# Weight sums of a seven-product block form, made in device memory by accumulating transfers

## The chip, the cores and the metric

The kernel runs on one core of a Trainium2 chip. The core has TensorE (PE: matrix products; PEld in the profile is its weight load), VectorE (DVE), ScalarE (ACT), GpSimd (POOL) and SyncE (SP, which here only issues transfers), each with its own queue of instructions, and 16 transfer (DMA) engines that all queues share. The metric is the device time of one execution in microseconds (us), less is better.

## The reference

Two layers of an encoder over 512 tokens of width 1024, in float32. Each layer adds three parts to x: a mixer of two kinds of attention, an attention over 256 memory tokens, and a feed-forward part. The change is in the last:

```python
def conv_ffn(h, w_up, conv_w, conv_b, w_down):
    u = h @ w_up
    up = jnp.pad(u, ((0, 0), (1, 1), (0, 0)))
    u = up[:, :-2] * conv_w[0] + up[:, 1:-1] * conv_w[1] + up[:, 2:] * conv_w[2] + conv_b
    gate, val = jnp.split(u, 2, axis=-1)
    return (jax.nn.silu(gate) * val) @ w_down

for l in range(DEPTH):                                   # DEPTH = 2
    x = x + hybrid_mixer(rms_norm(x, norm_mix[l]), w_in[l], ...)
    x = x + memory_cross_attention(rms_norm(x, norm_mem_q[l]), rms_norm(mem, norm_mem_kv[l]), ...)
    x = x + conv_ffn(rms_norm(x, norm_ffn[l]), w_up[l], conv_w[l], conv_b[l], w_down[l])
return rms_norm(x, norm_final)
```

`w_up` is 1024 x 5632: 2816 columns of "gate", then 2816 of "val". `w_down` is 2816 x 1024.

## The kernel before

Activations lie with channels on partitions: x is 8 tiles `xT` of 128 channels x 512 tokens. A float32 product is made of three products of rounded operands: each operand is split into a "hi" part (rounded, cast by ACT) and a "lo" part (the rest, a subtraction on POOL or DVE), and `mm3` multiplies hi by hi, hi by lo and lo by hi. Weights come from device memory in a fixed list, `plan`: each entry is loaded into one of three buffers `raw` by SP's queue, and split into `hi` and `lo` (four buffers each) before its use. SP issues the next load of the list when a `raw` buffer is free.

One layer takes about 620 to 650 us. First the mixer's attention runs: steps of 8 units of neighbourhood attention, then 16 of the grouped kind, with projections as filler between the steps (`weave`; `na_quanta(s)` is called once in each step s of the first kind). Then comes the attention over the memory tokens, and last the feed-forward part, in 22 chunks j of 128 gate and 128 val columns, with rows of `w_down` woven in from the second group on.

Chunks 0 to 5 are plain products. Chunks 6 to 21 ("blocks" in the text below, 16 per layer) are made by seven products of half size instead of eight. With the rows of `w_up` in two halves of 512, a11 and a12 are the upper and lower half of the gate columns and a21 and a22 those of the val columns; the tokens are in two halves of 256. The seven products need the weights a11, a12, a22 themselves and four sums of halves. Before the change the sums are made block by block from the two loaded `raw` tiles by four DVE instructions (lines 773, 774, 779 and 780), into buffers `sf`, which are then split like weights:

```python
DVE.tensor_add(both[:, :4], raw[:, :4], raw[:, 4:])                    # 773
DVE.tensor_sub(both[:, 4:], both[:, :4], sums["gate"][:, :4])          # 774
DVE.tensor_sub(both[:, :4], sums["gate"][:, 4:], sums.pop("s2"))       # 779
DVE.tensor_sub(both[:, 4:], sums["gate"][:, :4], sums["val"][:, :4])   # 780
```

The order of instructions on PE, ACT, DVE and POOL is not the written one: the class `Order` simulates the program with assumed durations and due times, and records an order for each engine (`InOrder` marks instructions that keep their written order). SP's transfers stay as written. Within an engine's queue everything runs in the recorded order: an instruction that waits holds all that are behind it.

Of the kernel before, what the change touches and what calls it, by code (L numbers as in the profile page):

```python
# [19 lines left out]
P = 128  # L20
S = 512
D = 1024
# [17 lines left out]
SCALED = 3  # L40
CUTS = 1
FIRST_ROWS = 2
# [20 lines left out]
LATE = 3600  # L63
N_SF = 2
N_RAW, N_W, N_R, N_T, N_S, AHEAD, N_WARM, N_FIRST = 3, 4, 21, 14, 24, 2, 7, (12, 24)
# [135 lines left out]

SLOTS = {"r": N_R, "t": N_T, "s": N_S, "mm": 4, "sc": 2, "tr": 2, "raw": N_RAW, "sf": N_SF, "hi": N_W, "lo": N_W, "xg": 2, "rep": 1}

# [8 lines left out]

DMA_ISSUE, DMA_NS, DMA_RATE, DMA_SHARE, DMA_GAP, DMA_MOST = 480.0, 2700.0, 310.0, 0.5, 150.0, 8

ROUNDS, REPLAYS, MARGIN, SHARES, STRETCH, SEED = 12, 4, 100.0, (0.0, 0.0, 0.5, 1.0, 2.0), 500, 4
# [9 lines left out]
class Step:  # L225
# [5 lines left out]
    def __init__(self, ins, index):  # L231
        self.ins, self.index, self.engine = ins, index, self.ENGINES[ins.engine]
        self.dma = type(ins).__name__ == "InstDMACopy"
        self.reads, self.writes = ([p for p in map(self.part, v) if p] for v in (ins.ins, ins.outs))
        self.names = list(dict.fromkeys(p[0] for p in self.writes + self.reads))
        self.bytes = 4.0 * self.count(ins.outs[0].bass_ap.ap) if self.dma else 0.0
        if self.dma and self.reads:

            self.bytes *= 1.5 if self.writes else 0.4
        self.busy, self.takes = self.times()  # L240
        self.sharing = self.shares()

    @staticmethod
# [6 lines left out]
    @classmethod  # L250
    def part(cls, arg):

        ap = getattr(arg, "bass_ap", None)
        if ap is None or not isinstance(ap.tensor, tile.Tile):
            return None
        row, dims = 1, [tuple(d) for d in ap.ap]
        for n in ap.tensor.shape[1:]:
            row *= n
        p0, at = divmod(ap.offset, row)
# [19 lines left out]
    def shares(self):  # L279

        what = type(self.ins).__name__
        if self.engine == "POOL":
            return bool(self.wide(self.reads)) and getattr(self.ins, "op", None) != ALU.pow
        if self.engine != "DVE" or what not in ("InstTensorTensor", "InstTensorScalarPtr") or self.banked(self.reads):
            return False
        return bool(self.reads) and max(p[4] for p in self.reads) > 1

    def times(self):

        ins, what = self.ins, type(self.ins).__name__  # L290
        if self.dma:
            return DMA_ISSUE, DMA_ISSUE
# [40 lines left out]
class Order:  # L333
# [107 lines left out]
    def due(self):  # L441

        start, now = {}, FIRST_PRODUCT
        for s in self.steps:
            if s.engine == "PE":
                start[s.index] = now - self.credit.get(s.index, 0.0)
                now += s.busy
        end = now + 1e4
        self.latest, queue = [end] * len(self.steps), end
        for s in reversed(self.steps):  # L450
            until = min([end] + [self.latest[j] - self.wait(s, self.steps[j]) for j in self.chain[s.index]])
            if s.engine == "PE":
                self.latest[s.index] = start[s.index]
            elif s.dma:
                queue = self.latest[s.index] = min(until - DMA_NS - s.bytes / DMA_RATE, queue - s.busy)
            else:
                self.latest[s.index] = min([until - s.takes] + [self.latest[j] for j in self.then.get(s.index, ())])

    def run(self, given=None, draw=None):
# [141 lines left out]
        while len(issued) < n or moving:  # L601
# [45 lines left out]
            for name in s.names:  # L647
# [4 lines left out]
                held.add(name)  # L652
            if s.dma:
                if not moving:
# [9 lines left out]
def encoder_kernel(ctx: ExitStack, tc: tile.TileContext, t: dict, out: bass.AP):  # L664
# [12 lines left out]
    spool = ctx.enter_context(tc.tile_pool(name="spool", bufs=N_S))  # L677
    psum = ctx.enter_context(tc.tile_pool(name="psum", bufs=2, space=PSUM))

    uid = [0]  # L680
# [38 lines left out]
    def raw_tile():  # L719
        key, loads, nk, ncol, eng = plan[len(raws)]  # L720
        if not loads:
            raws.append(None)
            return None, loads
        if eng[1:] == "x":
            raw = rtile((nk, ncol), F32)
        else:
            raw = wpool.tile([P, nk, ncol], F32, tag="raw", name=nm("raw"), bufs=N_RAW)
        raws.append(raw)
        return raw, loads
# [6 lines left out]
    def emit_split(act=ACT, cuts=2):  # L736
# [3 lines left out]
        raws[n] = None  # L740
        if key[0] in FORMS:
            ready.append(FORMS[key[0]](raw, act))
            return
        if key[0] in ("up", "down", "memq", "memo"):
            cuts = 1
        hi = wpool.tile([P, nk, ncol], F32R, tag="hi", name=nm("hi"))
        lo = wpool.tile([P, nk, ncol], F32R, tag="lo", name=nm("lo"))
        for i in range(cuts):
# [3 lines left out]
        ready.append((hi, lo))  # L752

    sums = {}

    def split_form(src, n, act, eng):
        hi = wpool.tile([P, 2 * n, P], F32R, tag="hi", name=nm("hi"), padded_shape=[P, KC, P])
        lo = wpool.tile([P, 2 * n, P], F32R, tag="lo", name=nm("lo"), padded_shape=[P, KC, P])
        act.copy(hi, src)  # L759
        for i in range(CUTS if eng is POOL else 1):  # L760
            c = slice(2 * n * i // CUTS, 2 * n * (i + 1) // CUTS) if eng is POOL else slice(0, 2 * n)
            eng.tensor_sub(lo[:, c], src[:, c], f(hi)[:, c])  # L762
        return hi, lo

    def form_gate(raw, act):
        sums["gate"] = raw
        return split_form(raw, 4, act, POOL)

    def form_sums(raw, act):
        sums["val"] = raw  # L770
        both = wpool.tile([P, KC, P], F32, tag="sf", name=nm("sf"), bufs=N_SF)
        sums["s2"] = both[:, 4:]
        DVE.tensor_add(both[:, :4], raw[:, :4], raw[:, 4:])
        DVE.tensor_sub(both[:, 4:], both[:, :4], sums["gate"][:, :4])  # L774
        return split_form(both, 4, act, DVE)

    def form_differences(raw, act):
        both = wpool.tile([P, KC, P], F32, tag="sf", name=nm("sf"), bufs=N_SF)
        DVE.tensor_sub(both[:, :4], sums["gate"][:, 4:], sums.pop("s2"))
        DVE.tensor_sub(both[:, 4:], sums["gate"][:, :4], sums["val"][:, :4])  # L780
        return split_form(both, 4, act, POOL)

    def form_val(raw, act):
        return split_form(sums["val"][:, 4:], 2, act, DVE)

    FORMS = {"gate": form_gate, "sums": form_sums, "diffs": form_differences, "val": form_val}

# [151 lines left out]
    qrs = [cpool.tile([P, 2 * NB], F32, name=f"qr{g}") for g in range(4)]  # L939

    def load_parameters():
        SP.dma_start(par[:, 0, 8:], t["par"][:, 0, 8:])
        SP.dma_start(par[:, 1], t["par"][:, 1])
        SP.dma_start(gfin, t["gfin"])

    ident = cpool.tile([P, P], F32, name="ident")
# [223 lines left out]
    for l in range(DEPTH):  # L1170
# [506 lines left out]

        def na_quanta(s):
            if l == 0 and s < 7:
                stat.step(1)  # L1680
# [158 lines left out]
        def convolve(j, us):  # L1839
            cs = []  # L1840
            for side in range(2):
                ch = side * NF + j
                u = us[side]
                w = [par[:, l, CW + i * 2 * NF + ch : CW + i * 2 * NF + ch + 1] for i in range(3)]
                cc = tmp()
# [42 lines left out]
        def token_forms():  # L1888


            made = {}
            for name, a, b in (("t1", (0, 1), (0, 0)), ("t2", (1, 1), "t1"), ("t3", (1, 1), (0, 1)), ("t4", (1, 0), "t2")):
                src = made[name] = rtile((4, HALF), F32)
                for i in range(2):
                    k = slice(2 * i, 2 * i + 2)
                    other = made[b][:, k] if isinstance(b, str) else quarter(*b)[i]
                    (POOL if name == "t3" else DVE).tensor_sub(made[name][:, k], quarter(*a)[i], other)
                xform[name] = hi, lo = [rtile((4, HALF)) for _ in range(2)]
                ACT.copy(hi, src)
                (POOL if name in ("t2", "t3") else DVE).tensor_sub(lo, src, f(hi))  # L1900
                yield
# [256 lines left out]
```

## Time and profile before

| | us |
|---|---|
| median of 3 runs (1311.10 to 1312.67) | 1311.57 |
| span of the profiled execution, first to last instruction | 1308.7 |
| TensorE busy in it | 1298.8 |
| DVE busy | 995.7 |
| ACT busy | 786.2 |
| POOL busy | 716.6 |

The profile is of one execution, and its span leaves out what lies around the program, so it stands 2.9 us under the median. The granted TensorE clock is 0.999 of full speed. Stages in the trace, in us from the start: attention of the first layer from about 39 to 235, memory attention to 325, its feed-forward part to 640; the second layer likewise from 640, its attention about 690 to 880, its feed-forward part from 975 to the end. "Busy" of TensorE is modelled for the ends of its matmuls, which overlap; the distance from one start to the next tells its pace. Rows of the profile name an instruction by source line, engine, operation, output<-inputs and shape, then x count, busy us and mean ns, and the idle time before it with what ended it. Rows by stretch give, behind the stretch and its length, busy us and count of PE, PEld, DVE, ACT and POOL, then the granted clock, the transfer engines' busy share and GB/s. Rows in order of time begin with the start and the length in us.

### The profile page before, as it was taken

The numbers are of one execution on the slowest core, as the hardware profiler recorded it, in microseconds if no ns is written. First come the engines' busy times: TensorE is split into PE (matmuls) and PEld (weight loads), VectorE is DVE, ScalarE is ACT, GpSimd is POOL, SyncE is SP. The second block draws the span as 40 slices with busy tenths as digits, with TensorE's granted clock in tenths as the row PEclk, the third lists the DMA queues.
The fourth block names the chain that finished last, engine by engine and source line by source line (L and its number), as shares of the span: only waits on it lengthen the run. The fifth ranks groups of instructions, "written<-read, shape, count | busy, mean of one in ns | idle before, by whom it ended". The sixth has DMA issues, their size and how long they took to land.

```text
span 1308.7 us, 20968 instructions
## 1 busy us (share of the span) xinstructions
PE 1298.8 (99%) x7595; PEld 1144.2 (87%) x7595; DVE 995.7 (76%) x1855; ACT 786.2 (60%) x1459; POOL 716.6 (55%) x518
## 2 busy tenths in 40 slices
PE   9999999999999999999999999999999999999998
PEld 8888888888789999999888888888888999999987
DVE  6559877675999888788535688776759999887874
ACT  6668876565555555555536678775645555555544
POOL 2757955727454454445746569656364544444443
PEclk9999999999999999999999999999999999999999
DMA  8734322313223433333455533223232333333341
GB/s 256 211 117 110 113 65 66 109 36 113 85 61 106 116 102 101 98 95 102 134 154 167 147 79 104 62 73 94 60 93 85 89 89 105 103 97 94 106 139 65
DMA packets 203464, 137.50 MB, mean 105 GB/s; under 512 B 5600, under 2 KB 192480, under 8 KB 203360
## 3 DMA queue, kind: packets, MB, share of 16 engines
q1 hardware_dynamic: 202944, 135.77, 35.4%
q8 instruction: 60, 0.98, 0.3%
q14 instruction: 44, 0.36, 0.1%
q10 hardware_dynamic: 416, 0.39, 0.1%
HBM read 126.18 MB, written 2.10 MB: 98 GB/s over the span
## 4 chain that ended last, share of the span: by engine, by line
PE 95%; DVE 2%; ACT 1%; issue 1%; DMA 1%; POOL 0%; POOLq 0%; SPq 0%; ACTq 0%; DVEq 0%
PE mm L104 65%; PE sc L104 22%; PE tr L104 4%; PE tr L1558 2%; PE tr L1403 1%; PE tr L1747 1%; DMA r<-in_memT 1%; DVE t L1853 0%; ACT hi L750 0%; PE tr L1473 0%; DVE r L1875 0%; DVE r L1052 0%; DVE xg L1884 0%; ACT r L1051 0%; DVE t L1461 0%
## 5 line engine op out<-in xcount | busy, mean ns | idle before, releaser
L751 POOL TENSOR_TENSOR lo<-raw,hi 128x512 fp32r<-128x512 f32 (+3 forms) x229 | 368.1, 1620 | 276.2 <-ACT hi L750 226.2
L104 PE MATMUL mm<-r,hi 128*128 128x512 f32 (+1 forms) x1344 | 387.2, 368 | 0.0
L104 PEld LDWEIGHTS mm<-r,hi 128*128 128x128 f32 x1344 | 238.0, 189 | 34.9
L104 PE MATMUL mm<-xg,hi 128*128 128x512 f32 (+1 forms) x960 | 266.3, 363 | 0.8 <-DVE xg L1884 0.4
L104 PE MATMUL mm<-r,lo 128*128 128x512 f32 (+1 forms) x704 | 251.0, 358 | 0.0
L750 ACT CAST hi<-raw 128x512 fp32r<-128x512 f32 (+3 forms) x233 | 167.5, 741 | 129.6 <-PE mm L104 39.5
L104 PEld LDWEIGHTS mm<-xg,hi 128*128 128x128 f32 x960 | 170.0, 189 | 28.0 <-ACT mm L1855 1.1
L104 PE MATMUL mm<-xg,lo 128*128 128x512 f32 (+1 forms) x480 | 173.4, 361 | 0.0
L104 PE MATMUL sc<-r,hi 128*128 128x256 f32 (+1 forms) x832 | 163.2, 292 | 0.0
L762 POOL TENSOR_TENSOR lo<-sf,hi 128x1024 fp32r<-128x1024 f32 x32 | 78.0, 2437 | 147.9 <-ACT hi L759 101.0
L104 PEld LDWEIGHTS mm<-r,lo 128*128 128x128 f32 x704 | 132.9, 189 | 20.0
L104 PEld LDWEIGHTS sc<-r,hi 128*128 128x128 f32 x832 | 133.6, 191 | 4.8
L104 PE MATMUL sc<-r,lo 128*128 128x256 f32 (+1 forms) x416 | 121.2, 292 | 0.0
L759 ACT CAST hi<-sf 128x1024 fp32r<-128x1024 f32 x64 | 67.1, 1048 | 87.6 <-DVE sf L774 38.7
L104 PE MATMUL mm<-hi,xg 128*128 128x512 f32 (+1 forms) x384 | 111.4, 360 | 0.0
L104 PEld LDWEIGHTS mm<-xg,lo 128*128 128x128 f32 x480 | 90.6, 189 | 14.1
L762 POOL TENSOR_TENSOR lo<-raw,hi 128x1024 fp32r<-128x1024 f32 x32 | 78.0, 2436 | 43.6 <-ACT hi L759 37.3
L1058 POOL TENSOR_SCALAR t<-t,s 128x512 f32<-128x512 f32 (+1 forms) x112 | 66.7, 611 | 52.4 <-DVE s L1542 28.5
L104 PEld LDWEIGHTS sc<-r,lo 128*128 128x128 f32 x416 | 79.6, 191 | 1.1
L104 PEld LDWEIGHTS mm<-hi,xg 128*128 128x128 f32 x384 | 68.1, 190 | 8.8
L104 PE MATMUL sc<-r,r 128*128 128x256 f32 (+1 forms) x352 | 73.6, 330 | 0.0
L104 PE MATMUL mm<-lo,xg 128*128 128x512 f32 (+1 forms) x192 | 68.5, 357 | 0.0
(213 smaller groups left out, 2626.8 us busy)
## 6 DMA issues: line engine op xcount, KB each, us to landing
raw<-in_w_up SPq DMA_DIRECT2D x88, 512.0 KB, 3.7
raw<-in_w_in SPq DMA_DIRECT2D x25, 512.0 KB, 4.6
raw<-in_w_down SPq DMA_DIRECT2D x32, 384.0 KB, 3.4
raw<-in_w_mem_kv SPq DMA_DIRECT2D x16, 512.0 KB, 4.2
raw<-in_w_down SPq DMA_DIRECT2D x24, 320.0 KB, 3.1
r<-in_bias SPq DMA_DIRECT2D x16, 384.0 KB, 4.7
r<-r SPq DMA_DIRECT2D x22, 256.0 KB, 3.5
raw<-in_w_in SPq DMA_DIRECT2D x18, 256.0 KB, 4.8
```

The source lines that it names most:

```text
L104: return self.engine.matmul(out, lhsT, rhs, **k)
L750: act.copy(hi[:, k], raw[:, k])
L751: (POOL if eng[0] == "P" else DVE).tensor_sub(lo[:, k], raw[:, k], f(hi)[:, k])
L759: act.copy(hi, src)
L762: eng.tensor_sub(lo[:, c], src[:, c], f(hi)[:, c])
L1058: eng.tensor_scalar(e, e, sums[:, col : col + 1], 1.0, op0=ALU.mult, op1=ALU.mult)
L1403: PE.transpose(tr[:, (2 * i + c) * P : (2 * i + c + 1) * P], es[j][:, i, c * P : (c + 1) * P], ident)
L1558: PE.transpose(tr[:, k * P : (k + 1) * P], es[j][:, k * P : (k + 1) * P], ident)
L1747: PE.transpose(tr[:, (2 * c + i) * P : (2 * c + i + 1) * P], e[:, i, c * P : (c + 1) * P], ident)
```

## The change

The sums are made once per layer and for all 16 blocks, in device memory. Two tensors per layer, `sums` and `diffs`, each 1024 x 2048, are filled half by half (512 x 2048, 4.19 MB): ScalarE's queue issues a plain copy of one half of a `w_up` part into it, and POOL's queue then issues a transfer that adds a second operand to what is there (`accum_op`). The third sum adds onto the first, so its source is the half made before. The four pairs are written in steps 0 to 3 of the neighbourhood attention of the same layer. The feed-forward part then loads `sums` and `diffs` like weights, and of the val columns only the lower half (a22). [...] The `sf` buffers go. `Order` learns of the new transfers ("far": landing 45 us after the issue, a POOL issue 1.5 us).

```diff
+    made = [[dpool.tile([D, WIDE], F32, name=f"dr_{n}{l}") for n in ("sums", "diffs")] for l in range(DEPTH)]
+    def make_form(l, n, act):
+        w, half = t["w_up"][l], D // 2
+        gate, val = slice(P * PLAIN, D_FF), slice(D_FF + P * PLAIN, 2 * D_FF)
+        sums, diffs = made[l]
+        a11, a12, a21, a22 = w[:half, gate], w[half:, gate], w[:half, val], w[half:, val]
+        dst, base, more = [(sums[:half], a21, a22), (sums[half:], a11, sums[:half]),
+                           (diffs[half:], a11, a21), (diffs[:half], a12, sums[half:])][n]
+        act.dma_start(dst, base)
+        nc.gpsimd.dma_start(dst, more, accum_op=ALU.add, max_dma_last_dim=4 * 2048)
...
         if j >= PLAIN:
             cols(("gate", j), t["w_up"][l], 0, KC, P * j, P)
-            cols(("sums", j), t["w_up"][l], 0, KC, D_FF + P * j, P)
-            plan.append((("diffs", j), [], KC, P, "P"))
-            plan.append((("val", j), [], KC, P, "P"))
+            cols(("sums", j), made[l][0], 0, KC, P * (j - PLAIN), P, "D")
+            cols(("diffs", j), made[l][1], 0, KC, P * (j - PLAIN), P)
+            cols(("val", j), t["w_up"][l], KC // 2, KC // 2, D_FF + P * j, P, "D")
...
         def na_quanta(s):
+            if s < 4:
+                make_form(l, s, ACT_IN_ORDER)
...
+                if side and j >= PLAIN:
+                    w = [minus[:, l, i, j : j + 1] for i in range(3)]
...
+                    if name == "t4":
+                        DVE.tensor_add(src[:, k], one, other)
+                    elif name == "t2":
+                        DVE.tensor_sub(src[:, k], other, one)
...
+                if name in ("t1", "t4"):
+                    ACT.mul(hi, src, -1.0)
+                    DVE.scalar_tensor_tensor(lo, src, -1.0, f(hi), op0=ALU.mult, op1=ALU.subtract)
...
+            elif s.far:
+                self.latest[s.index] = until - FAR_NS
...
-    nc = bacc.Bacc("TRN2", target_bir_lowering=False, num_devices=1, dynamic_dma_scratch_size=1024)
+    nc = bacc.Bacc("TRN2", target_bir_lowering=False, num_devices=1, dynamic_dma_scratch_size=4096)
```

How the order moves. First ScalarE's queue early in the first layer's attention, before and after; `r` here are projected values, `hi` casts of weights, `t` and `s` the softmax's tiles:

```order
L1054 ACTIVATE r_392<-mm_396,s_319 128x4x64 x2
L750 CAST hi_509<-raw_382 128x512 x2
L750 CAST hi_580<-raw_390 128x512
L1054 ACTIVATE r_393<-mm_449,s_319 128x4x64
L750 CAST hi_580<-raw_390 128x512
L1054 ACTIVATE r_393<-mm_449,s_319 128x4x64
```

```order
L1059 ACTIVATE r_401<-mm_405,s_328 128x4x64 x2
L79 DMA dr_sums_78<-in_w_up 512x2048
L784 CAST hi_520<-raw_391 128x512 x2
L784 CAST hi_591<-raw_399 128x512
L1059 ACTIVATE r_402<-mm_458,s_328 128x4x64
L784 CAST hi_591<-raw_399 128x512
L79 DMA dr_sums_78<-in_w_up 512x2048
```

The first two copies have come in, the rest stands as it was; the first of these casts starts at 39.46 us in the trace of before.

POOL's queue further on in the same attention, before and after; L1058 (after: L1063) scales softmax rows, L1468 (L1473) turns projected queries, L1078 (L1083) splits an output:

```order
L1078 TENSOR_TENSOR r_1273<-t_1050,r_1273 128x512
L1468 TENSOR_TENSOR t_1283<-t_1283,t_1282 128x8x32 x2
L1468 TENSOR_TENSOR t_1357<-t_1357,t_1356 128x8x32
L1058 TENSOR_SCALAR t_1305<-t_1305,s_1304 128x256
L1058 TENSOR_SCALAR t_1306<-t_1306,s_1304 128x256 x2
```

```order
L1083 TENSOR_TENSOR r_1290<-t_1067,r_1290 128x512
L1473 TENSOR_TENSOR t_1300<-t_1300,t_1299 128x8x32 x2
L714 DMA dr_diffs_79<-in_w_up 512x2048
L1473 TENSOR_TENSOR t_1374<-t_1374,t_1373 128x8x32
L1063 TENSOR_SCALAR t_1323<-t_1323,s_1321 128x256
L1063 TENSOR_SCALAR t_1322<-t_1322,s_1321 128x256
L1063 TENSOR_SCALAR t_1323<-t_1323,s_1321 128x256
```

The accumulating transfer of the third pair, which waits for the third copy, has come in ahead of the turning of a query and of the scalings behind it.

SP's queue in the feed-forward part of the first layer, before and after:

```order
L81 DMA raw_4773<-in_w_up 128x8x128
L81 DMA raw_4805<-in_w_down 128x6x128
L81 DMA raw_4844<-in_w_up 128x8x128
L81 DMA raw_4937<-in_w_up 128x8x128
L81 DMA raw_4969<-in_w_down 128x6x128
```

```order
L79 DMA raw_4586<-in_w_up 128x8x128
L79 DMA raw_4618<-dr_sums_78 128x8x128
L79 DMA raw_4650<-dr_diffs_79 128x8x128
L79 DMA raw_4686<-in_w_up 128x4x128
L79 DMA raw_4716<-in_w_down 128x6x128
```

A block's two loads of `w_up` (512 KB each) have become four, the last of them of half size.

More of the change, by code (lines that the diff above doesn't have):

```diff
@@ L241, in __init__, with in_dram @@
         self.sharing = self.shares()
+    @classmethod
+    def in_dram(cls, arg):
+        ap = getattr(arg, "bass_ap", None)
+        return ap is not None and isinstance(ap.tensor, tile.Tile) and cls.kind(ap.tensor.name) == "dr"
     @staticmethod
@@ L258, in part @@
             row *= n
+        if cls.kind(ap.tensor.name) == "dr":
+            first, last = ap.offset // row, (ap.offset + sum(step * (n - 1) for step, n in dims)) // row
+            return ap.tensor.name, first, last + 1 - first, 1, cls.count(dims[1:])
         p0, at = divmod(ap.offset, row)
@@ L290, in times @@
         ins, what = self.ins, type(self.ins).__name__
+        if self.dma and self.engine == "POOL":
+            return FAR_POOL, FAR_POOL
         if self.dma:
@@ L652, in run @@
                 held.add(name)
-            if s.dma:
+            if s.far:
+                landed.add(j)
+                over_(s, t, t + FAR_NS)
+            elif s.dma:
                 if not moving:
@@ L752, in emit_split @@
         ready.append((hi, lo))
[L754 to L786, printed above, removed]
     def prepare_w(ahead):
@@ L944, in load_parameters @@
         SP.dma_start(gfin, t["gfin"])
+        for i in range(DEPTH):
+            taps = par[:, i, CW : CW + 6 * NF].rearrange("p (i c) -> p i c", i=3)
+            DVE.tensor_scalar(minus[:, i], taps[:, :, NF:], -1.0, None, op0=ALU.mult)
     ident = cpool.tile([P, P], F32, name="ident")
```

42 lines of the change are left out of this document (24 added, 18 removed).

## The prediction

> **What bounds the kernel now.** I read the page's busy times first, then the busy time by stretch, then the long stretch of the feed-forward blocks (400 to 640 us) by instruction form, since the change takes work from the vector engine (DVE) there.
>
> ```profile
> PE 1298.8 (99%) x7595; PEld 1144.2 (87%) x7595; DVE 995.7 (76%) x1855; ACT 786.2 (60%) x1459; POOL 716.6 (55%) x518
> ...
> 400.00:640.00 240.00, 240.00 (x1625) 222.99 (x1624) 196.36 (x308) 127.92 (x192) 113.96 (x56) 1.00 0.34 100
> ...
> L104 PE MATMUL mm<-r,hi 128*128 128x512 f32 x280 | 86.9, 392 | 0.0
> L104 PE MATMUL mm<-r,lo 128*128 128x512 f32 x140 | 54.5, 389 | 0.0
> ...
> 408.95 1.44 PE tr L104 x12
> ...
> 619.87 20.20 PE mm L104 x89
> ```
>
> The matmul ends are modelled, so "240 of 240 us busy" alone proves little; the pitch does. The last two rows come from the chain of waits: twelve 256-wide products in 1.44 us, 0.120 us each, and 89 of 512 in 20.20 us, 0.227 us each. The stretch holds 1625 matmuls, of which 280 + 140 = 420 are 512 wide and 1205 are 256 wide (all its other forms): 420 x 0.227 + 1205 x 0.120 = 95.3 + 144.6 = 239.9 us in 240.0. TensorE waits for nothing there, and no product is added or taken. So whatever leaves DVE in these blocks is worth 0 us.
>
> **The change, part by part.** *The sums leave DVE.* Four groups go:
>
> ```profile
> L773 DVE TENSOR_TENSOR sf<-raw 128x512 f32<-128x512 f32 x32 | 60.0, 1874 | 6.8 <-DMA raw<-in_w_up 6.8
> L774 DVE TENSOR_TENSOR sf<-sf,raw 128x512 f32<-128x512 f32 x32 | 23.0, 717 | 0.1
> L779 DVE TENSOR_TENSOR sf<-raw,sf 128x512 f32<-128x512 f32 x32 | 32.6, 1019 | 0.0
> L780 DVE TENSOR_TENSOR sf<-raw,raw 128x512 f32<-128x512 f32 x32 | 21.8, 681 | 0.0
> ```
>
> That is 60.0 + 23.0 + 32.6 + 21.8 = 137.4 us of DVE, all beside a gapless TensorE: 0 us. The negated tokens and taps change operations one for one and add two small ones: 0 us, under the same cover.
>
> *More loads per block.* A block (an up-chunk j of 6 and more) now loads 0.5 + 0.5 + 0.5 + 0.25 MB where it loaded 1 MB; 32 blocks, 24 MB more. The bound there is the three "raw" buffers.
>
> ```profile
> raw<-in_w_up SPq DMA_DIRECT2D x88, 512.0 KB, 3.7
> raw<-in_w_down SPq DMA_DIRECT2D x32, 384.0 KB, 3.4
> ...
> L759 ACT CAST hi<-sf 128x1024 fp32r<-128x1024 f32 x64 | 67.1, 1048 | 87.6 <-DVE sf L774 38.7 <-PE sc L104 36.3 <-PE mm L104 7.1
> L762 POOL TENSOR_TENSOR lo<-sf,hi 128x1024 fp32r<-128x1024 f32 x32 | 78.0, 2437 | 147.9 <-ACT hi L759 101.0 <-PE mm L104 47.0
> L773 DVE TENSOR_TENSOR sf<-raw x14: 693/2098/2745, 401.0 to 602.1; 128x512 f32<-128x512 f32 x14
> ```
>
> One is held for landing, cast and subtraction: 3.7 + 1.05 + 2.44 = 7.2 us for gate and for differences, about 6.0 for sums (subtraction on DVE, half as long), under 5 for the quarter, about 6 for each of 1.3 to 1.6 w_down rows. That is 33 to 35 us per block over three buffers, 11 to 12 us; the last row's 14 blocks start 201.1/13 = 15.5 us apart. It fits with a quarter to spare: 0 us.
>
> *The sums in device memory.* Per layer four plain copies on ScalarE's queue and four accumulating transfers on POOL's, 512 x 2048 x 4 B = 4.19 MB each. Issuing costs ScalarE 8 x 0.5 us (the SP row of 50.82 us below has two issues in 1.00 us). POOL has no such row; I bound its 8 issues by that 0.5 us and by its longest row above, 2.4 us each, 4 to 19 us in all, and take the low end as the nearest in kind. The places at which they stand have 1.8 to 4.7 us of idle POOL beside them (rows below): 0 us on the path. What costs is where they run and what waits for them. No copy from device memory to device memory stands in this trace. One copy's time c, if it had all 16 transfer engines to itself, is bounded by these rows, the first three from 3.1 to 3.4 us, where the engines were full, the last two from the whole span:
>
> ```profile
> DMA packets 139, 0.11 MB, mean 362 GB/s; under 512 B 14, under 2 KB 110, under 8 KB 139
> ...
> q10 hardware_dynamic: 109, 0.05, 56.3%
> q1 hardware_dynamic: 30, 0.06, 52.5%
> ...
> q1 hardware_dynamic: 202944, 135.77, 35.4%
> q8 instruction: 60, 0.98, 0.3%
> ```
>
> At 362 GB/s c is 11.6 us. All loads together (0.354 x 1308.7 = 463 us of all engines for 135.77 MB, 293 GB/s) make it 14.3 us; the instruction queue, the one with large packets (16 KB), 3.9 us for 0.98 MB, 250 GB/s, 16.8 us. The copied rows are 8 KB long and the loads' mostly 512 B, so I go above the loads' mean, between the first two: c = 13 us. The q10 and q1 rows are the only overlap of two queues: 0.05 against 0.06 MB, half each. So I let queues share equally.
>
> *Where they run.* By the new order the first copy is issued just ahead of the first of these ScalarE rows, and in layer 1 just behind the second; the others follow within 31 us.
>
> ```profile
> 39.46 1.14 ACT L750 CAST hi<-raw 128x512 fp32r<-128x512 f32 x2 [0.54 <-PE mm L104]
> ...
> 688.66 0.61 ACT L750 CAST hi<-raw 128x512 fp32r<-128x512 f32 x1
> ...
> 39.00:62.00 23.00, 23.00 (x122) 19.71 (x121) 10.51 (x30) 16.80 (x41) 17.93 (x19) 1.00 0.90 250
> 62.00:82.00 20.00, 20.00 (x113) 17.33 (x112) 13.19 (x38) 12.16 (x35) 10.68 (x13) 1.00 0.63 197
> 82.00:110.00 28.00, 28.00 (x158) 24.30 (x157) 19.59 (x57) 18.82 (x51) 21.13 (x23) 1.00 0.49 142
> 690.00:720.00 30.00, 30.00 (x156) 25.51 (x156) 17.26 (x47) 19.20 (x49) 18.82 (x21) 1.00 0.59 182
> 734.00:757.00 23.00, 22.70 (x126) 19.45 (x125) 16.34 (x45) 16.76 (x44) 18.59 (x20) 1.00 0.60 170
> ```
>
> The next-to-last figure is the transfer engines' share already in use: 0.90, 0.63, 0.49 and 0.59, 0.60. The copies land in the busiest stretches of each layer, so they get a half and the loads fall behind. For the loads that is nearly covered. The weight loaded at 50.8 us is split from 59 us and first multiplied at 72.0 us:
>
> ```profile
> raw<-in_w_in SPq DMA_DIRECT2D x18, 256.0 KB, 4.8
> ...
> 50.82 1.00 SPq L81 DMA_DIRECT2D raw<-in_w_in  x2
> 58.98 1.14 ACT L750 CAST hi<-raw 128x512 fp32r<-128x512 f32 x2
> 60.30 2.54 POOL L751 TENSOR_TENSOR lo<-raw,hi 128x512 fp32r<-128x512 f32 x2
> 72.01 0.62 PE L104 MATMUL mm<-hi,xg 128*128 128x512 f32 x2
> ```
>
> It lands by about 56 us (4.8 us to land, the median of its group in the first row), so it can be 2.8 + 9.2 = 12 us late. At half the engines the 0.90 x 17 = 15 us of transfers due by 56 us take 30 us: 13 us late, 1 us over. I count +1 us.
>
> *Who waits for them.* Each accumulating transfer stands in POOL's queue and waits there for its copy; every subtraction and softmax scaling behind it waits too. The first stands ahead of the row at 83.91 us, 44 us after its copy: covered. The second (into "diffs") stands ahead of 115.39 us, and ahead of 758.42 us in layer 1, behind three copies:
>
> ```profile
> 83.91 1.30 POOL L1078 TENSOR_TENSOR r<-t,r 128x512 fp32r<-128x512 f32 x1 [4.42 <-ACT r L1077]
> 115.39 0.74 POOL L1468 TENSOR_TENSOR t<-t,t 128x256 f32<-128x256 f32 x1 [4.71 <-DVE t L1461]
> 116.16 1.65 POOL L1058 TENSOR_SCALAR t<-t,s 128x256 f32<-128x256 f32 x3
> 120.20 0.60 PE L1403 MATMUL tr<-ident,t 128*128 128x128 f32 x4
> ...
> 737.57 2.55 POOL L751 TENSOR_TENSOR lo<-raw,hi 128x512 fp32r<-128x512 f32 x2 [4.38 <-issue]
> 758.42 1.30 POOL L1078 TENSOR_TENSOR r<-t,r 128x512 fp32r<-128x512 f32 x1 [1.80 <-ACT r L1077]
> 764.51 1.39 POOL L1058 TENSOR_SCALAR t<-t,s 128x256 f32<-128x256 f32 x3 [2.87 <-DVE s L1506]
> ```
>
> Layer 0: from 39.5 to 84 us the copies get half, 22.3 us of work; from 84 us, beside the loads and the first accumulation, a third, 10.4 us by 115.4. Done: 32.7 us; needed: 3 x 13 = 39. With POOL stopped TensorE soon stops and with it the loads, so the copies share with the accumulation alone, half again: 6.3 x 2 = 12.6 us late. The scalings end at 117.8 and TensorE transposes their result at 120.2, 2.4 us of slack: 10 us on the path. Layer 1: half from 688.7 to 737.6 (24.5 us), a third until 761.8 (764.51 less the 2.7 us that POOL has ahead of it; 8.1 us): 32.6 us, and again 10 us. The third and fourth accumulation stand 38 and 70 rows further on in POOL's queue and find their copies landed: 0 us.
>
> Sum: 0 + 0 + 0 + 1 + 10 + 10 = 21 us on the profiled span of 1308.7, which lies 2.9 us under the median of the runs, 1311.57 (time outside the span, kept as it is): 1332.6 us, say 1332. With c = 11.6 the two waits shrink to 2 us each (1317), with 14.3 they are 18 each (1349).
>
> [...]
>
> **The rivals.**
>
> *The copies drain in time.* With c under 10.9 us (32.7/3) POOL never waits, and the loads' lag stays inside its 12 us: 0 to 2 us, 1311 to 1314. The 362 GB/s row is near; the 0.90 row is against it. Chance 0.20, four fifths of it within 0.2%.
>
> *Copies as slow as the instruction queue's.* c = 16.8 us: (50.4 - 32.7) x 2 - 2.4 = 33 us per layer, 1311.6 + 66 + 1 = 1379 us. [...] Chance 0.17.
>
> *Loads starve by packet.* From 39 to 62 us the loads are 4254 packets, 266 per engine; three copies are 96 rows of 8 KB per engine. Were packets taken in strict turns, each would pass one load packet (0.90 x 23/266 = 0.08 us): 96 x (13/32 + 0.08) = 47 us for 96 of the 266. The load of 50.8 us, about the 200th of them, would come at 39 + 47 + 104 x 0.08 = 94 us, 38 late, 26 after its slack, and about half that in layer 1, where the stretch is 0.59 full; POOL's waits then vanish: 1311.6 + 39 = 1350 us.
>
> ```profile
> DMA packets 4254, 5.74 MB, mean 250 GB/s; under 512 B 375, under 2 KB 3319, under 8 KB 4252
> ```
>
> The q10 row (109 packets against 30) speaks against it. Chance 0.10. [...]
>
> *The blocks become load-bound.* If casts and subtractions queue 1.5 us or more per load, three buffers no longer suffice and each of 32 blocks loses about 1 us: 1344 us. 15.5 against 11 to 12 us speaks against it. Chance 0.07.
>
> *Faster.* Place: the attention, where the recorded order is made anew around the transfers. Price: TensorE's visible gaps from 95 to 975 us, such as the 23.00 - 22.70 = 0.3 us above. It decides only if the waits hidden under modelled ends shrink by more than 2.6 us in all, with c under 10.9. About 1308 us, chance 0.04. The vector engine's relief can't do it, since TensorE has no gap there.
>
> **How the numbers follow.** The forecast has 0.42, the rivals 0.20, 0.17, 0.10, 0.07 and 0.04. 0.2% (2.6 us) is about what a measurement of this kernel can tell from no change. Faster: 0.04. Same: 0.16 of the drained case, plus 0.02 of late loads that stay inside their slack: 0.18. Slower: 0.78. The range runs from the drained case (1310) to just over the slow copies (1385); below and above it stays about 0.15. The forecast's own range is 1317 to 1349.
>
> **What would show it.** Right: from 400 to 640 us TensorE again 240 of 240 us; two POOL waits of some 10 us, at about 115 and 765 us, released by a transfer into "dr_sums" or "dr_diffs"; the copies landing 25 to 50 us after issue; the 39 to 62 us stretch at a share near 1. Wrong: no POOL wait and loads at their old 4 to 5 us (copies cheap); loads of 20 us and more (starved); gaps in the blocks.

## The result, and the profile after

| | before | after |
|---|---|---|
| median, us | 1311.34 (1310.54 to 1312.67, 4 runs) | 1418.92 (1416.20 to 1420.08, 4 runs) |
| span of the profiled execution | 1308.7 | 1414.3 |
| TensorE busy in it | 1298.8 | 1324.3 |
| mean granted clock | 0.999 | 0.969 |

The change makes the kernel slower by a factor of 1.082 (95% interval 1.0805 to 1.0836), 107.6 us; the prediction had 1332 in a range that ended at 1385. Two of the medians below include one disturbed execution, which moves them by less than 0.3 us; the trace of the kernel without transfers is of such an execution (1414 us at a clock of 0.85) and is not read. The page of the changed kernel, in the parts that the prediction spoke of (queues: packets, MB, share of 16 engines; issues: size and median us from issue to landing; SPq, ACTq and POOLq are the queues of SP, ScalarE and POOL as issuers of transfers):

```profile
PE 1324.3 (94%) x7595; PEld 1158.5 (82%) x7595; DVE 843.6 (60%) x1729; ACT 788.1 (56%) x1459; POOL 721.3 (51%) x526
...
q1 hardware_dynamic: 253120, 160.94, 39.1%
q0 software_dynamic: 4224, 33.55, 11.6%
q10 hardware_dynamic: 4640, 33.95, 6.9%
...
dr_sums<-in_w_up ACTq DMA_DIRECT2D x4, 4096.0 KB, 24.0
dr_diffs<-in_w_up ACTq DMA_DIRECT2D x4, 4096.0 KB, 19.3
...
dr_sums<-in_w_up POOLq DMA_DIRECT2D x2, 4096.0 KB, 26.8
```

The same 7595 matmuls are 25.5 us longer busy, and TensorE is idle 90.0 us instead of 9.9: 25.5 + 80.1 = 105.6 us, the whole difference of the spans. q10 holds the eight copies, q0 the eight additions. A copy takes 0.069 x 1414.3 / 8 = 12.2 us of all engines, an addition 0.116 x 1414.3 / 8 = 20.5 us, for the same 4.19 MB. By stretch (us busy of PE, PEld, DVE, ACT, POOL; granted clock; transfer share; GB/s):

```profile
36.00:120.00 84.00, 54.18 (x254) 44.11 (x252) 22.95 (x63) 27.27 (x71) 29.12 (x31) 0.83 0.94 309
440.00:680.00 240.00, 240.00 (x1675) 225.12 (x1674) 131.93 (x257) 130.95 (x194) 114.26 (x55) 1.00 0.54 153
744.00:860.00 116.00, 81.01 (x395) 67.91 (x394) 45.46 (x128) 48.47 (x129) 47.00 (x51) 0.84 0.95 282
```

The middle row is the blocks: DVE fell from 196.36 to 131.93 us in a stretch of the same length, and TensorE is as gapless as before. The outer rows are the two attentions while the copies run (and, from 815 us, the additions): a third of the time TensorE stands. The chain of waits in the first stretch and its like in the second (start, length, what was waited for) names who is late:

```profile
40.02 25.89 DMA raw<-in_w_in
...
86.62 30.87 DMA t<-in_memT
...
744.82 17.07 DMA dr_sums<-in_w_up
761.96 14.83 DMA r<-in_bias
776.81 16.18 DMA dr_diffs<-in_w_up
```

Two of the five are ordinary loads that took 26 and 31 us. The third and fourth belong together: a copy issued at 744.82 lands, and only then, at 761.96, does SP issue the load of a bias. SP's waits between 36 and 330 us (total, times, longest):

```profile
SPq L79 <- DMA dr_sums<-in_w_up: 26.5, 2, 13.5
...
SPq L79 <- DMA dr_diffs<-in_w_up: 7.9, 1, 7.9
```

No load reads those tensors there; before, SP waited for landings 2.9 us in all in the same stretch. The instructions of the trace say why. Each transfer of SP and ScalarE counts its landing on one of eight completion semaphores (counters that others can wait for; here numbers 100, 102, 103 and 106 to 110), taken in turn over both queues (394 of the 413 steps from one issue to the next go to the next number), and an issue waits until the transfer that had its semaphore before has landed (406 of the 414 transfers have such a forerunner, and none was issued ahead of its landing); POOL's eight additions count on 111 to 118:

| issued, us | queue | transfer | semaphore |
|---|---|---|---|
| 38.10 | ScalarE | first copy | 109 |
| 40.97 | ScalarE | second copy | 100 |
| 42.74 | SP | load `r<-r`, the last for 13.5 us | 108 |
| 56.27 | SP | load `r<-r` | 109, waited for |
| 70.89 | SP | load `r<-r` | 100, waited for |

The copies' last packets were moved at 53.9 and 69.9 us, and the last counts of their landing came at 56.25 and 70.87 us. So copies that landed 18.2 and 29.9 us after their issue stopped SP, and with it every load behind.

And POOL, whose two waits were the forecast:

```profile
120.33 1.38 POOL L1063 TENSOR_SCALAR t<-t,s 128x256 f32<-128x256 f32 x3
121.66 1.22 POOL L714 DMA_DIRECT2D dr_sums<-in_w_up  x1
```

There is no idle time ahead of the addition. POOL, itself held up by late weights, came to its first addition at 121.66 us instead of some 84, when both copies into "sums" had long landed.

### The profile page after: what moved, and what is told of

Same layout as the page of the kernel before. It is cut to its first block, busy times and chain, and to the rows that moved or that the text cites. A ratio compares the mean times of both kernels' runs of the same rounds, so it can differ in the third digit from the quotient of the medians.

```text
span 1414.3 us, 20974 instructions
## 1 busy us (share of the span) xinstructions
PE 1324.3 (94%) x7595; PEld 1158.5 (82%) x7595; DVE 843.6 (60%) x1729; ACT 788.1 (56%) x1459; POOL 721.3 (51%) x526
## 4 chain that ended last, share of the span: by engine, by line
PE 78%; DMA 12%; DVE 3%; POOL 2%; ACT 2%; issue 1%; SPq 0%; POOLq 0%; ACTq 0%
PE mm L102 52%; PE sc L102 19%; PE tr L102 4%; DMA raw<-in_w_in 4%; DMA raw<-in_w_mem_q 3%; DMA t<-in_memT 2%; PE tr L1563 2%; POOL lo L785 1%; DMA dr_sums<-in_w_up 1%; DMA dr_diffs<-in_w_up 1%; DMA r<-in_bias 1%; PE tr L1408 1%; PE tr L1754 0%; ACT hi L784 0%; DVE t L1863 0%
## 5 line engine op out<-in xcount | busy, mean ns | idle before, releaser
L785 POOL TENSOR_TENSOR lo<-raw,hi 128x512 fp32r<-128x512 f32 (+3 forms) x293 | 521.4, 1789 | 538.3 <-ACT hi L784 486.7
L784 ACT CAST hi<-raw 128x512 fp32r<-128x512 f32 (+3 forms) x361 | 288.2, 812 | 269.3 <-DMA raw<-in_w_in 68.9
L102 PE MATMUL mm<-xg,hi 128*128 128x512 f32 (+1 forms) x960 | 271.1, 368 | 3.2 <-ACT xg L1006 2.2
L102 PE MATMUL mm<-hi,xg 128*128 128x512 f32 (+1 forms) x384 | 117.9, 378 | 19.1 <-ACT t L1467 16.0
L102 PEld LDWEIGHTS mm<-hi,xg 128*128 128x128 f32 x384 | 72.3, 201 | 30.2 <-ACT t L1467 16.3
L102 PE MATMUL sc<-r,r 128*128 128x256 f32 (+1 forms) x352 | 76.7, 340 | 18.4 <-ACT t L1386 18.4
L1063 POOL TENSOR_SCALAR t<-t,s 128x512 f32<-128x512 f32 (+1 forms) x112 | 67.0, 618 | 45.7 <-DVE s L1547 26.8
L1950 DVE TENSOR_TENSOR tr<-mm,t 128x256 f32<-128x256 f32 x32 | 13.9, 433 | 111.5 <-PE mm L102 111.5
L785 DVE TENSOR_TENSOR lo<-raw,hi 128x1024 fp32r<-128x1024 f32 (+1 forms) x68 | 66.5, 978 | 20.2 <-ACT hi L784 20.1
L102 PEld LDWEIGHTS sc<-r,r 128*128 128x128 f32 x352 | 55.0, 197 | 25.7 <-ACT t L1386 19.8
L1863 DVE SCALAR_TENSOR_TENSOR t<-sc,minus,t 128x504 f32<-128x504 f32 (+1 forms) x128 | 56.1, 478 | 31.4 <-ACT t L1856 30.7
```

The source lines that it names most:

```text
L102: return self.engine.matmul(out, lhsT, rhs, **k)
L784: act.copy(hi[:, k], raw[:, k])
L785: (POOL if eng[0] == "P" else DVE).tensor_sub(lo[:, k], raw[:, k], f(hi)[:, k])
L1063: eng.tensor_scalar(e, e, sums[:, col : col + 1], 1.0, op0=ALU.mult, op1=ALU.mult)
L1863: DVE.scalar_tensor_tensor(cc[:, dst], u[:, src], wi, cc[:, dst], op0=ALU.mult, op1=ALU.add)
L1950: DVE.tensor_add(b[:, halves[1]], second, u2)
```

## The experiments

Times are medians; "above before" is against the kernel before, measured beside each (1310.7 to 1311.3). Where the additions are left out, so are the sums; the blocks then multiply other numbers by the same work.

**Nothing but the blocks.**

```diff
-        act.dma_start(dst, base)
-        nc.gpsimd.dma_start(dst, more, accum_op=ALU.add, max_dma_last_dim=4 * 2048)
...
-            cols(("sums", j), made[l][0], 0, KC, P * (j - PLAIN), P, "D")
-            cols(("diffs", j), made[l][1], 0, KC, P * (j - PLAIN), P)
+            cols(("sums", j), t["w_up"][l], 0, KC, D_FF + P * j, P, "D")
+            cols(("diffs", j), t["w_up"][l], 0, KC, P * j, P)
```

> The changed kernel without its sixteen transfers between device-memory tensors; the blocks load the same number of bytes from w_up in place of the sums (the sums are left out). Theory (the transfers starve the loads of the attention; the blocks cost nothing): 1309 to 1314 us, no gap of TensorE in the blocks, granted clock back to 1.00. Rival (the 24 MB more of loads, the token forms or the newly made order cost something): 1325 us and more.

1310.87 us, ratio 0.9983 (0.9964 to 1.0003), granted clock 0.999. The 24 MB of further loads and the token forms (`token_forms` moves signs into the tokens, `minus` into the convolution's taps, so that additions alone make the sums) cost nothing, and 137 us less of DVE bring nothing. So the whole 107.6 us comes with the sixteen transfers, and taking the sums off DVE can gain nothing here: with sums for nothing the kernel is where it was. (The order is recorded anew for each kernel; what the order that the transfers bring costs without them was not tested. In the traces TensorE falls behind the kernel before in the stretches where transfers run, and not in the blocks.)

**The copies without the additions, and then in pieces of 512 bytes.**

```diff
-        nc.gpsimd.dma_start(dst, more, accum_op=ALU.add, max_dma_last_dim=4 * 2048)
```

> The changed kernel with the eight plain copies and without the eight accumulating transfers. Of the 106 us that TensorE stands longer in the changed kernel, about 60 lie in the stretches in which the copies run and 45 in those of the accumulations. Theory (each transfer costs on its own): 1365 to 1378 us. Rival (the price is in the chain of copy and accumulation): 1311 to 1320 us. Rival (copies alone do it): 1400 us and more.

```diff
-        act.dma_start(dst, base)
+        act.dma_start(*(v.rearrange("k (c p) -> c k p", p=P) for v in (dst, base)))
```

> As the kernel with the eight plain copies alone, but each copy in pieces of 512 bytes instead of rows of 8 KB: the same bytes at the same places. Theory (a transfer engine takes the queues' packets in turn, so that a 512-byte packet of a load waits for an 8 KB packet): loads issued beside the copies land in 8 to 15 us instead of 18 to 30, the copies take 25 to 30 us, 1320 to 1345 us. Rival (it is the volume, or SP standing until a copy has landed): no better than with 8 KB rows, 1365 us and more.

1381.59 and 1369.20 us, 70.5 and 58.1 above before. The copies are two thirds of the loss, the additions the other 37. The landing of loads while copies run, in the kernel before, the changed one and the one with 512-byte pieces, one row pair each:

```profile
r<-in_bias SPq DMA_DIRECT2D x5, 384.0 KB, 5.8
...
raw<-in_w_in SPq DMA_DIRECT2D x3, 512.0 KB, 6.5
```

```profile
r<-in_bias SPq DMA_DIRECT2D x6, 384.0 KB, 19.7
...
raw<-in_w_in SPq DMA_DIRECT2D x3, 512.0 KB, 23.6
```

```profile
r<-in_bias SPq DMA_DIRECT2D x6, 384.0 KB, 8.1
...
raw<-in_w_in SPq DMA_DIRECT2D x3, 512.0 KB, 7.6
```

5.8 and 6.5 us became 19.7 and 23.6, and 8.1 and 7.6 with small pieces: the same bytes moved beside them, so it is not the volume. The packets that each queue moved while the first copy of the changed kernel ran (40.1 to 53.9 us) show what it is:

```profile
q10 hardware_dynamic: 520, 4.19, 86.3%
q1 hardware_dynamic: 483, 0.50, 11.5%
```

520 packets against 483: about one of each queue in turn, and 8 KB (0.31 us in the median record) stands against 1 KB (0.05 us). The queues shared packets here, not time: the loads got 11.5%. This was a rival of the prediction, with a chance of 0.10.

Yet the time fell by 12 us only, not to the expected 1345: the rival's number (1365 and more) came, by SP's wait. The small pieces land later than the rows (29 and 27 us at the median instead of 24 and 19), and ScalarE, in its issue of the second copy behind the 8192 pieces of the first, stood 16 us. The chain goes through the landing of this copy, for which SP waited:

```profile
40.95 16.41 ACTq L79 DMA_DIRECT2D dr_sums<-in_w_up  x1
...
40.95 34.66 DMA dr_sums<-in_w_up
75.63 0.46 SPq L79
...
SPq L79 <- DMA dr_sums<-in_w_up: 30.8, 2, 19.5
```

**The copies from POOL's queue**, in rows of 8 KB.

```diff
+        POOL_IN_ORDER.dma_start(dst, base, max_dma_last_dim=4 * 2048)
```

> The eight plain copies alone, issued by POOL's queue at the same places of the program instead of ScalarE's, so that SP's loads share no completion semaphore with them. Theory (packets in turn decide): SP no longer waits for a copy's landing, but the loads still take 15 to 30 us beside one; 1350 to 1378 us. Rival (SP's wait for the copies' landing decides): 1311 to 1330 us. And the packet of 8 KB: 309 ns as on ScalarE's queue if the 629 ns of the accumulating transfers is the price of the addition, 629 ns if it is that of the queue.

1358.74 us, 47.7 above before, 22.9 less than from ScalarE's queue. SP waits for no copy now, yet loads that meet one are late: the 256 KB ones of "raw" took 17.3 us at the median (from 40 to 127 us), though those of 512 KB only 5.3. So both the packets and SP's wait are real. The copies also stand at other times here, so 22.9 us is no clean price of SP's wait. This queue's row:

```profile
q0 software_dynamic: 4224, 33.55, 6.8%
```

0.068 x 1358.8 / 8 = 11.5 us a copy on the queue on which an addition took 20.5: the difference is the price of adding, not of this queue.

**Pieces of 2 KB**, three kernels, as `v.rearrange("k (c p) -> c k p", p=512)`: on ScalarE's queue, on POOL's in two halves, and in the spread kernel below.

> The eight plain copies alone on ScalarE's queue, in pieces of 2 KB. With 512-byte pieces the loads landed in 6 to 8 us instead of 13.7 on average, yet ScalarE stood 13 to 16 us in the issue of every second copy, and SP still waited 30 us in each layer for copies to land. Theory (three prices: packets in turn, ScalarE's issue of too many pieces, SP's wait for a shared semaphore): with 2 KB pieces ScalarE issues in under 1 us, loads land in 8 to 11 us, SP still waits 25 to 30 us per layer; 1335 to 1356 us. Rival (SP's wait is the whole price): 1365 us and more.

> The eight plain copies alone on POOL's queue, in pieces of 2 KB, each copy in two halves. Theory: none of the three prices is left but a milder turn of packets (loads in 8 to 11 us instead of 14 with 8 KB rows on this queue), and SP waits for no copy: 1318 to 1338 us. Rival (the volume itself fills the transfer engines where the loads need them): 1350 us and more, as with 8 KB rows on this queue (1358.7).

> As the kernel with the pairs spread, and the plain copies in pieces of 2 KB (the accumulating transfers stay in 8 KB rows). Theory: within 5 us of the spread kernel with 8 KB rows, and not above it, since the accumulating transfers, 21 us each, delay loads more than the copies; 1311 to 1322 us. Rival (the copies are what still costs): more than 5 us below it.

1584.12, 1616.95 and 1561.88 us: far above all that was expected, by a fault of my pieces. In the first of them, from 60 to 100 us:

```profile
60.00:100.00 40.00, 11.65 (x52) 9.67 (x52) 6.41 (x22) 5.40 (x15) 3.91 (x5) 0.66 0.28 107
```

The transfer share is 0.28 while a copy runs, 0.28 x 16 = 4.5 or about four of sixteen engines, and ScalarE's next issue took 38.69 us. The outermost dimension of these copies counts 4; with 512-byte pieces it counts 16, and there the copies alone filled 81.4% of the engines' time (42 to 57 us). That the count of 4 is the cause is my estimate from these two shares; no run varied it alone. These runs say nothing on packets.

**One copy at a time**, in steps 0, 3 and 6 of the neighbourhood attention and step 1 of the grouped one, in rows of 8 KB and in 512-byte pieces; then in steps 2, 6, 10 and 14 of the grouped attention.

```diff
-            if s < 4:
-                make_form(l, s, ACT_IN_ORDER)
+            if s in (0, 3, 6):
+                make_form(l, s // 3, ACT_IN_ORDER)
```

> The eight plain copies alone on ScalarE's queue in rows of 8 KB, but apart: in steps 0, 3 and 6 of the neighbourhood attention and step 1 of the grouped one, so that no two are on the way at once (no additions; the sums are left out). Theory (packets in turn): every load that meets a copy lands as late as the copy, 10 to 17 us; 1335 to 1370 us, less than back to back (1381.6). Rival (only copies queued behind each other cost): 1311 to 1325 us.

> As the kernel with copies apart, in pieces of 512 bytes. ScalarE then issues each in under 1 us, since none is queued behind another. Theory (packets in turn): loads beside a copy land in 6 to 8 us, and what is left is SP's wait for a shared semaphore, which the slack of the loads covers in part: 1311 to 1335 us, at least 15 us below the 8 KB rows. Rival (the volume, or SP's wait, is the price): within 5 us of the 8 KB rows.

```diff
+        def gqa_quanta(s):
+            if s in (2, 6, 10, 14):
+                make_form(l, s // 4, ACT_IN_ORDER)
```

> The eight plain copies alone on ScalarE's queue, rows of 8 KB, in steps 2, 6, 10 and 14 of the grouped attention, where SP issues only one load in 4 to 5 us and a load waits 4 to 25 us in its buffer. Theory (a copy costs what it delays a load beyond its waiting time, by packets in turn and by the shared semaphore): less than the 38 us of the same copies apart in the early attention, 1315 to 1335 us. Rival (the volume costs wherever it runs): 1345 to 1382 us.

> The same late places, pieces of 512 bytes. Theory: loads land in 6 to 8 us, SP issues too few transfers during a copy to meet its semaphore, and nothing is left to pay: 1309 to 1318 us. Rival (the volume, or another cost of the copies): 1330 us and more.

| copies alone | 8 KB rows | 512-byte pieces |
|---|---|---|
| back to back, as in the change | 1381.59 (+70.5) | 1369.20 (+58.1) |
| one at a time, early | 1348.91 (+38.0) | 1334.46 (+23.6) |
| one at a time, late | 1332.52 (+21.5) | 1316.16 (+5.2) |

At one place the packet size alone is worth 14.4 and 16.4 us; it was expected to be 15 at least, and is 14.4 at the early one. What is left early with small pieces is mostly SP's wait, as the chain of that kernel and SP's row show for the first layer:

```profile
38.78 22.97 DMA dr_sums<-in_w_up
61.81 0.46 SPq L79
```

```profile
SPq L79 <- DMA dr_sums<-in_w_up: 17.1, 1, 17.1
```

In that layer the 400th matmul starts 15.1 us later than before, of 23.6 us in all. The 7 us that the second layer loses were not traced to one wait. Late, where SP issues a load in 4 to 5 us, the row is gone from SP's waits, and the same 33.6 MB of copies cost 5 us (1.0034, 1.0021 to 1.0047). There, with room on the engines (52.7% of their time for the copies and 23.3% for the loads from 120 to 235 us), the volume cost no more than that.

**The whole change, moved or cut.** First the four pairs later and apart (steps 5 and 13 of the grouped attention, step 3 of the memory attention, chunk 2); then every transfer in four pieces of 1 MB, the copies one in each step, the additions behind the subtractions of the later weights; then the same with those subtractions kept in order.

> The whole changed kernel, with all sixteen transfers, rows of 8 KB and the same queues, but the four pairs of a layer are issued later and one at a time: in steps 5 and 13 of the grouped attention, in step 3 of the memory attention and ahead of chunk 2 of the feed-forward part, the assumed landing 30 us instead of 45. There a load waits 10 to 28 us in its buffer for its cast, and has some 10 us more until its product. Theory (a transfer costs only what it delays a load beyond that): 1311 to 1326 us. Rival (each transfer costs by its volume or by SP's wait wherever it runs): 1360 us and more.

> The whole changed kernel with each of its sixteen transfers cut into four of 128 rows (1 MB): the copies go one by one through the sixteen steps of the grouped attention, the accumulating ones one by one behind the subtractions of the weights of the memory attention and the plain chunks. Theory (a load is delayed by what is left of the transfer it meets, here 3.5 us of a copy and 5.3 us of an accumulation, and at most some 16 us where three follow each other, against 15 to 35 us of waiting in its buffer): 1309 to 1318 us. Rival (the volume costs wherever it runs, 34 MB copied and 34 MB added, some 65 to 75 us as in the spread kernel): 1360 us and more.

> The whole changed kernel in pieces of 1 MB as before, with the accumulating pieces now kept behind single subtractions of POOL, from the late grouped attention to the middle of the plain chunks, so that two at most are issued together (before, groups of three and four kept the transfer engines full for 35 us and TensorE stood 16 and 17 us behind them). Theory (a load is delayed by the transfers that it meets, and only what exceeds its waiting time costs): 1320 to 1345 us. Rival (the volume costs wherever it runs): 1365 us and more.

1382.10, 1379.30 and 1426.43 us: far above what I expected of each. By themselves these three spoke for the rival, that volume costs wherever it runs. The chain of the first, in its first layer, holds a load behind a pair, and the last addition itself: chunk 2 was so late a place that the blocks' loads waited for their data, SP 28.5 us for the last addition (in the second layer 31.01 and 24.05 us):

```profile
195.97 35.45 DMA raw<-in_w_out
...
392.45 22.84 DMA dr_diffs<-dr_sums
```

The second one where it loses most:

```profile
340.00:350.00 10.00, 4.74 (x21) 3.57 (x19) 0.27 (x1) 0.00 (x0) 0.00 (x0) 1.00 1.04 217
350.00:360.00 10.00, 0.00 (x0) 0.00 (x0) 0.00 (x0) 1.49 (x3) 0.36 (x1) 0.50 1.03 236
```

The pieces had not stayed apart: the recorded order let POOL issue six additions of 1 MB from 323.4 to 337.0 us, which filled the engines until 359 (shares of 1.03 to 1.05 from 330 to 360 us). A place in the code is no place in time. In the third kernel each addition has a subtraction in order ahead of it, and loads still stood behind the additions:

```profile
235.77 22.02 DMA raw<-in_w_mem_q
...
276.66 22.44 DMA raw<-in_w_mem_o
```

Why it is slower than the second was not taken apart; the order forced on POOL may have its part.

**Additions behind late copies**, back to back by the order's choice, and then kept apart.

```diff
+        act.dma_start(*(v.rearrange("k (c p) -> c k p", p=P) for v in (dst, base)))
...
-FAR_NS, FAR_POOL = 45000.0, 1500.0
+FAR_NS, FAR_POOL = 25000.0, 1500.0
```

> The whole changed kernel with the copies late and in 512-byte pieces, and the accumulating transfers in 8 KB rows behind them, from the late grouped attention into the memory attention (assumed landing 25 us instead of 45). Theory (the copies then cost nothing, the accumulating transfers keep a load packet waiting 629 ns each and delay a load by up to 21 us, beyond its waiting time by a few us each): 1325 to 1355 us, all above 1318 due to the additions. Rival (accumulating transfers are as harmless there): 1309 to 1318 us. Rival (they cost what the whole change costs): 1380 us and more.

1429.36 us, 113 above its copies alone. Two additions ran from 225 to 270 us without a break. What the queues moved in 25 us of that (243 to 268), and the load that was issued in it:

```profile
q0 software_dynamic: 607, 4.84, 92.8%
q1 hardware_dynamic: 607, 0.31, 6.2%
q10 hardware_dynamic: 607, 0.31, 4.1%
...
raw<-in_w_mem_q SPq DMA_DIRECT2D x1, 512.0 KB, 26.4
```

Three queues, 607 packets each, as in strict turns. Spread over 16 engines that is 607 / 16 = 38 rounds in 25 us, 0.66 us a round, of which the loads' 512 bytes get 6%. By that estimate a load of 512 KB in 512-byte rows, 64 packets on each engine, needs 64 x 0.66 = 42 us, or as long as the additions last; the load in the row took 26.4 us, and the three issued between 225.5 and 269.8 us took 34.0 at the median.

```diff
+            if s in (2, 9, 17):
+                make_form(l, {2: 0, 9: 1, 17: 2}[s], "base")
+            if s in (6, 13):
+                make_form(l, {6: 0, 13: 1}[s], "more")
...
+            if s == 3:
+                make_form(l, 2, "more")
+            if s == 7:
+                make_form(l, 3, "base")
```

> The whole changed kernel, copies late and in 512-byte pieces, and the four accumulating transfers of a layer kept apart from each other and from the next copy: at steps 6 and 13 of the grouped attention, step 3 of the memory attention and chunk 2. In the late full kernel two of them ran back to back (45 us), and a load of the memory attention that met both landed after 34 to 40 us: its 64 packets of 512 bytes on each transfer engine, one to every 0.629 us packet of the addition, give 64 x 0.656 = 42 us. Theory (a load is held until the transfer is done, 21 us for one, and only what exceeds its waiting time is paid): 1318 to 1345 us. Rival (an accumulating transfer costs some 14 us wherever it runs): 1400 us and more.

1361.03 us, 50.1 above before and 68 below the kernel with additions back to back: the rival (14 us each, 1400 and more) falls, and my 1345 was too low as well. The chain in the first layer holds the second copy, slowed beside the first addition (37.19 us; without additions the late copies into "sums" landed after 18.8 at the median), and a load (in the second 34.86 and 18.48 us, and a load of "w_up" of 23.03):

```profile
183.15 37.19 DMA dr_sums<-in_w_up
...
234.00 21.44 DMA raw<-in_w_mem_q
...
POOL dr_sums L79 <- DMA dr_sums<-in_w_up: 12.1, 1, 12.1
```

The last row is the kind of wait that the prediction had forecast: POOL stood, with the scalings behind it, until that copy landed, and SP waited 13.8 us for a copy. How the 45 us above the late copies alone (1316.16) split over eight additions was not taken apart.

## Why the prediction was wrong

That the kernel would get slower came true, but not by the path that was forecast: 20 of the 21 us stood on two waits of POOL that measured 0 us.

*The blocks: right.* DVE's sums were worth 0 us and the further loads too: 240.00 of 240 us of TensorE, and 1310.87 us without the transfers.

*The copy's price c = 13 us: right.* 12.2 us of all engines; beside loads 4.19 MB in 13.8 us, 304 GB/s.

*"So I let queues share equally": wrong, and the step that failed first.* It was read from one stretch of 0.3 us. The queues shared packets, so an 8 KB row left a load of 512-byte or 1 KB rows 6 to 12% of the time (6.2 and 11.5% above). From this came "1 us over" for the late loads; in the changed kernel loads land after 26 and 31 us, and ScalarE and POOL stand behind them in order (ScalarE 11.83 us ahead of a cast at 66.01 us, and 68.9 us in all for loads of `w_in`). The rival that had the mechanism put 39 us on it; copies alone, apart, in 8 KB rows, cost 38.0, by SP's wait as well, so the near match is in part luck.

*SP's queue: not in the sum at all.* The forecast asked who waits for POOL and never what a 4 MB transfer does to transfers behind it that share its semaphore. SP waited 34 us from 36 to 330 us for copies whose data no load needed there.

*The additions: mis-sized.* They were priced as copies that share time. An addition took 20.5 us of the engines instead of 12.2, and held an engine 0.63 us a packet in the median record; by the rows of the late additions it is 0.61 against 0.04 for a load's packet of 512 bytes (92.8% and 6.2% of 25 us x 16, over 607). In the changed kernel they cost 37 us (1418.92 less 1381.59), back to back 113.

*Two POOL waits of 10 us: wrong, 0 us.* They assumed that POOL keeps its old times. Late loads delayed POOL more than the copies: its first addition came at 121.66 us, and both copies into "sums" had landed by 70.87.

*The range.* Its upper end was the slow copy (1385), a bound on the size of one term; the errors were two terms that were missing.

## What to carry to other kernels

Price a large background transfer by what it does to the small ones beside it. Here about one packet of 8 KB went for each of theirs (520 against 483) and left them 11.5% of the time, so ask for the size of both rows before the bandwidth, and compare the delay with the time that a load would have waited in its buffer anyway. Ask too which transfers share a semaphore with a long one: here SP and ScalarE shared eight in turn, and SP stood 34 us in one layer until copies had landed. Before moving work off an engine, look whether TensorE has a gap where it stood; here it had none, and nothing could be won.

## What the runs showed of the hardware

- An accumulating transfer between device-memory tensors took 20.5 us of all engines for 4.19 MB in the changed kernel, against 11.5 us for a plain one from the same queue in the kernel with POOL's copies alone.
- With three queues busy the 16 engines moved as many packets of each (607, 607, 607 in 25 us, late additions), and with two about as many (520 and 483 in 13.8 us, changed kernel).
- While a copy whose outermost dimension counts 4 ran, the transfer share was 0.28 (60 to 100 us of the first kernel with 2 KB pieces), as if on four engines.
- A stall cost more than itself. From 60 to 68 us of the changed kernel TensorE was busy for 1.07 us, and in the 4 us after it the granted clock was 0.50:

```profile
60.00:68.00 8.00, 1.07 (x6) 0.50 (x4) 0.00 (x0) 1.99 (x4) 1.29 (x2) 0.73 1.00 343
68.00:72.00 4.00, 3.81 (x13) 2.71 (x12) 3.30 (x10) 0.61 (x2) 2.58 (x4) 0.50 0.75 252
```

The slower clock is most of the 25.5 us by which the same matmuls were longer busy: in slices of 2 us, TensorE's busy time times what the clock lacked of full speed adds up to 21.5 us.
